# A decoder layer step on one core: gated attention's decays by products from level to level, the decay's input columns loaded once, no arithmetic on GpSimd

## The chip, the cores and the metric

The kernel runs on one core of a Trainium2 chip. The core has TensorE (PE in the profile), VectorE (DVE), ScalarE (ACT), GpSimd (POOL) and SyncE (SP), and 16 DMA engines. Each engine executes its own instructions in order. The metric is the device time of one execution in microseconds; the median of three runs of the kernel before is 2003.5 us (2000.65 to 2004.73).

## The reference, cut to what matters

One layer is computed for 256 prompt tokens and 8 single-token samples, 264 columns in all, with D_MODEL 2048, everything in fp32. The input projection `x @ w_in` gives queries, keys, values, gates and a low-rank (16 columns) input of the decay. The gated attention is the part that the change touches most:

```python
log_a = log_sigmoid(a_lr @ w_gla_a2 + b_gla_a2) / 16.0
...
bc = cumsum(ac, axis=2)                              # log decay, summed over the tokens
decay = exp(where(tri, bc_t - bc_s, -inf))
scores = einsum('bhtk,bhsk,bhtsk->bhts', qc, kc, decay)
o = einsum('bhts,bhsv->bhtv', scores, vc) + einsum('bhtk,bhkv->bhtv', qc * exp(bc), S)
S = exp(b_last) * S + einsum('bhsk,bhsv->bhkv', kc * exp(b_last - bc), vc)
```

The score of tokens t and s is thus the sum over the 256 channels of a head of q_t * k_s * (product of the decays of the tokens after s up to t). There are 4 heads. Beside it run a short gated convolution and a cross-attention into 256 memory tokens; the three are projected, gated and summed, projected by w_o, normed, and followed by a convolutional FFN (D_FF 5504) and a second norm. Each matrix is read once from HBM.

## The kernel before, in words

**Matmuls.** A weight matrix is taken in groups of 512 output columns and granules of two k-tiles (2 x 128 rows, 512 KB). `granule` loads one with a DMA on SP's queue into a staging tile `ws` (4 buffers), casts it on ScalarE into `wh` and takes the remainder on VectorE into `wl` (L277, 3 buffers each). `group` then issues three products for every k-tile and 128 columns, wh·xh, wh·xl and wl·xh (L302 to L304), 264 columns wide and accumulated in PSUM. A granule is 24 such products.

**Order.** After every granule `tick` counts a clock and runs small work that the program has queued: due items of `later(n, f)`, then either a piece of a head's generator (`gens`, a piece ends at a `yield n`, which also says how many ticks the next one waits) or one unit of the queue (`pop`, a unit with loads that were issued two units ahead). Which ticks of a group may do so is one line (L234): with 8 granules those with 5, 4, 2 and 1 granules left, with 4 granules those with 1 and 0 left. All loads of weights and of units go to SP's queue in one order; each waits there for its buffer.

**The places around the change.**
- Memory attention: 16 `key_unit`s multiply a 512 KB piece of the key cache with a row of queries that is read back from DRAM (`dq`, L430) by VectorE (L439); then softmax, `value_unit`s. The prompt's logits (L554), their softmax on VectorE and ScalarE and transposes on TensorE (L568) follow the two memory projections. The projections' results are written to HBM by two DMAs each on GpSimd's queue (L529).
- The decay's input: `group([(win, A0, 32)] * 3, 16, xh, xl, gk=8)` reads the same 32 columns of w_in three times into 96 columns (rows of 128 bytes), in two granules of 8 k-tiles; 48 products.
- `head`: the log decays of a head are summed by a scan (L650); at each of seven lengths l = 1, 2, 4 ... 64 GpSimd subtracts them at the middle of blocks of 2l (L699, L702), ScalarE takes exp (L706), VectorE multiplies with keys and queries (L714, L717), TensorE forms a 128 x 128 product (L679) which VectorE copies where a mask is set (L688). Two more exponents give the decay between the halves and to the end (L736 to L752).
- `sum_rows` (48 calls) transposes 32 x 32 blocks and reduces on VectorE; once in 8 calls `product` sums over four partition groups by four products with shifted identity strips (L473).
- GpSimd also adds `merged` (L1014), the residual (L1087) and a part of the norm's sum (L1135), and its queue loads the FFN's past rows (L1059, two DMAs, rows of 512 bytes).

Of the kernel before, what the change touches and what calls it, by code (L numbers as in the profile page):

```python
# [34 lines left out]
def layer_kernel(ctx, tc, x_prompt, x_sample, mem_prompt, cache_mem_k, cache_mem_v, state_gla, state_conv,  # L35
# [81 lines left out]
    strip = sb.tile([P, 7 * 32], F32, name="strip")  # L117
    vcol = sb.tile([P, NV], F32, name="vcol")
    fcol = sb.tile([P, 172], F32, name="fcol")

    quads = lambda c: strip[:, 96 - 32 * c:224 - 32 * c]

    def constants():
        G.memset(strip, 0.0)
        for a in range(4):
            G.tensor_tensor(strip[:, 96:128], strip[:, 96:128], ident[:, 32 * a:32 * a + 32], ALU.add)
# [102 lines left out]
    def tick(left, n):  # L229

        clock[0] += 1
        with queued_behind():
            due()
            if left in ((1, 0) if n == 4 else (5, 4, 2, 1) if n == 8 and share[2] == 1 else range(2, n)):  # L234
                can = gens and clock[0] >= rest[0]
                if can and (not queue or share[0] < 3):
                    share[0] += 1
                    part()
                elif queue and clock[0] >= share[1]:
                    share[0:2] = [0, clock[0] + share[2]]  # L240
                    pop()
# [217 lines left out]
    def sum_rows(sums, b, z, dst, after=None):  # L459
# [9 lines left out]
        def product():  # L469
            pt = small()  # L470
            o = pt[:, 0:4 * NS].rearrange("p (b j) -> p b j", b=NS)
            for c in range(4):
                T.matmul(o, quads(c), R.rearrange("p b (j c) -> p b j c", c=4)[:, :, :, c], start=(c == 0), stop=(c == 3))  # L473
# [35 lines left out]
    for name, w, dst in (("k", w_mem_k[0], o_mk), ("v", w_mem_v[0], o_mv)):  # L509
# [18 lines left out]
        for m in range(2):  # L528
            G.dma_start(dst[0, 0, m * P:(m + 1) * P].rearrange("m h d -> m (h d)"), mt_[m])  # L529
# [48 lines left out]
    flush()  # L578
# [7 lines left out]
    wr = big(F32, (96, 1024))  # L586
    wa2 = big(F32R, (96, 1024))
    G.memset(wr, 0.0)
    for i in range(3):
        G.dma_start(wr[32 * i:32 * i + 16], w_gla_a2[0])  # L590
    pa, = group([(win, A0, 32)] * 3, 16, xh, xl, gk=8)
    aT = sb.tile([96, NT], F32R, name="aT")
    S.copy(aT, pa[0:96])
# [17 lines left out]
    def head(h, q, k, vf):  # L611
        qk = t2(F32, (P, 2, NP))
        G.tensor_tensor(qk, q[:, :, 0:NP], k[:, :, 0:NP], ALU.mult)
        G.tensor_tensor(qk[:, 0], qk[:, 0], qk[:, 1], ALU.add)
# [13 lines left out]
        def decays_of_samples():  # L628

            S.activation(eas[:, h], la[:, :, NP:NT], AF.Exp, scale=1.0 / 16.0)  # L630
            dot = tiny((P, 2, NS))
            V.tensor_mul(dot, qks[:, 0, h], qks[:, 1, h])
            later(1, lambda: (V.tensor_mul(qas[:, h], qks[:, 0, h], eas[:, h]), own_key(dot)))

        def own_key(dot):
            pz = small()
            for kt in range(2):
                T.matmul(pz[:, 0:NS], onesm, dot[:, kt], start=(kt == 0), stop=(kt == 1))
# [7 lines left out]
        yield 3  # L646

        L = t2(F32, (P, 2, NP))
        for kt in range(2):
            V.tensor_tensor_scan(L[:, kt], smask, la[:, kt, 0:NP], 0.0, ALU.mult, ALU.add)  # L650
        L4 = L.rearrange("p k (c t) -> p (k c) t", t=64)
        Lc = L.rearrange("p k (c t) -> p k c t", t=64)
        D1 = t2(F32, (P, 2, NP))
        D4 = D1.rearrange("p k (c t) -> p (k c) t", t=64)
        Dc = D1.rearrange("p k (c t) -> p k c t", t=64)
        V.tensor_sub(D4, L4[:, :, 63:64].to_broadcast([P, 8, 64]), L4)
        Tc = lambda c: Lc[:, :, c, 63:64]
# [11 lines left out]
        G.memset(sc[:, 3], 0.0)  # L669
# [6 lines left out]
        def gram(E):  # L676
            pg = small()
            for kt in range(2):
                T.matmul(pg[:, 0:P], E[:, kt, 0:P], E[:, kt, P:NP], start=(kt == 0), stop=(kt == 1))  # L679
# [4 lines left out]
        def level():  # L684

            li, E = pending.pop(0)
            pg = gram(E)
            V.copy_predicated(sc[:, 3], masks[:, li], pg[:, 0:P])  # L688

        halves = lambda a: [a[:, :, e * P:(e + 1) * P] for e in range(2)]  # L690

        def exponents(li, l, E):
            blk = lambda a: a.rearrange("p k (b w) -> p k b w", w=2 * l)
            Eh, Lh, qh = ([blk(t) for t in halves(a)] for a in (E, L, q))
            if l < 64:
                Lv = L.rearrange("p k (b w) -> p (k b) w", w=2 * l)
                Ev = E.rearrange("p k (b w) -> p (k b) w", w=2 * l)
                ref = Lv[:, :, l - 1:l].to_broadcast([P, 2 * NP // (2 * l), l])
                G.tensor_tensor(Ev[:, :, 0:l], ref, Lv[:, :, 0:l], ALU.subtract)  # L699
                for e in range(2):  # L700
                    ref = Lh[e][:, :, :, l - 1:l].to_broadcast([P, 2, P // (2 * l), l])
                    G.tensor_tensor(Eh[1 - e][:, :, :, l:2 * l], Lh[e][:, :, :, l:2 * l], ref, ALU.subtract)  # L702

            def decay():
                if l < 64:
                    S.activation(E, E, AF.Exp, scale=1.0 / 16.0)  # L706
                    return
                Ec = E.rearrange("p k (c t) -> p (k c) t", t=64)
                S.activation(Ec[:, 0::2], D4[:, 0::2], AF.Exp, scale=1.0 / 16.0)
                for e in range(2):  # L710
                    S.activation(Eh[1 - e][:, :, 0, l:], Lh[e][:, :, 0, l:], AF.Exp, scale=1.0 / 16.0)

            def products():
                V.tensor_mul(blk(E)[:, :, :, 0:l], blk(E)[:, :, :, 0:l], blk(k[:, :, 0:NP])[:, :, :, 0:l])  # L714
                for e in range(2):
                    u = Eh[1 - e][:, :, :, l:2 * l]
                    V.tensor_mul(u, u, qh[e][:, :, :, l:2 * l])  # L717
                pending.append((li, E))

            later(1, decay)  # L720
            later(2, products)

        for li, l in enumerate(LEVELS):
            yield 1
            exponents(li, l, t2(F32, (P, 2, NP)))
            if len(pending) > 1:
                level()
        yield 2

        E = t2(F32, (P, 2, NP))  # L730
        RD = t2(F32, (P, 2, NP))
        Rc = RD.rearrange("p k (c t) -> p k c t", t=64)
        Ec = E.rearrange("p k (c t) -> p k c t", t=64)
        T23 = tiny((P, 2, 1))
        bc = lambda a: a.to_broadcast([P, 2, 64])
        G.tensor_tensor(T23, Tc(2), Tc(3), ALU.add)  # L736
        G.tensor_tensor(Ec[:, :, 0], Dc[:, :, 0], bc(Tc(1)), ALU.add)
        G.tensor_copy(Ec[:, :, 1], Dc[:, :, 1])
        G.tensor_copy(Ec[:, :, 2], Lc[:, :, 2])
        G.tensor_tensor(Ec[:, :, 3], Lc[:, :, 3], bc(Tc(2)), ALU.add)  # L740
        G.tensor_tensor(RD[:, :, 0:P], E[:, :, 0:P], T23.to_broadcast([P, 2, P]), ALU.add)
        G.tensor_tensor(Rc[:, :, 2], Dc[:, :, 2], bc(Tc(3)), ALU.add)
        G.tensor_copy(Rc[:, :, 3], Dc[:, :, 3])

        def decay_halves():
            S.activation(E, E, AF.Exp, scale=1.0 / 16.0)
            S.activation(RD, RD, AF.Exp, scale=1.0 / 16.0)

# [653 lines left out]
```

## Time and profile before

| what | value |
|---|---|
| runs | 2004.73, 2000.65, 2003.5 us |
| profiled execution, its own time | 2005.06 us |
| its span from first to last instruction | 2003.3 us |
| busy: TensorE, VectorE, ScalarE, GpSimd | 1984.9, 1296.7, 986.3, 164.1 us |
| mean granted TensorE clock | 0.996 |
| VectorE's longest group, the remainders of L277 | 802.6 us in 651 |

A row of the waits reads: engine, tile and line <- what it waited for: us in total, times, the longest. A row of the timeline or of the chain: start in us, duration, engine, line, what. A row of the windows: stretch, its length, then busy us and number of instructions (x) for PE, PEld (weight loads), DVE, ACT and POOL, the granted TensorE clock (1.00 is full), the busy share of the DMA engines, GB/s. In grouped lines "x48 | 5.9, 274" is the count, busy us and mean ns. SPq and POOLq rows are DMA issues; the duration of merged rows ("x2") holds the waits between them.

### The profile page before, as it was taken

What the parts mean: (1) busy time and instruction counts of PE and PEld (TensorE: products, weight loads), DVE (VectorE), ACT (ScalarE), POOL (GpSimd) and SP (SyncE); (2) the same over time, 40 slices, a digit from 0 to 9 for tenths busy, and PEclk for the clock granted to TensorE, in tenths of its full rate; (3) what the DMA queues carried; (4) which work ended last, traced back from release to release, by engine and by line L of the source; (5) the groups of instructions that cost most, each with busy time, mean ns of one, the idle gap of its engine ahead of it and who ended that gap; (6) DMA issues with size and microseconds to landing.
All of it is one profiled execution on the core that took longest, in us unless ns stands there. A gap on an engine that the chain in (4) does not pass through costs nothing.

```text
span 2003.3 us, 38161 instructions
## 1 busy us (share of the span) xinstructions
PE 1984.9 (99%) x15721; PEld 1950.6 (97%) x15721; DVE 1296.7 (65%) x1947; ACT 986.3 (49%) x1348; POOL 164.1 (8%) x240
## 2 busy tenths in 40 slices
PE   9998999999999999999999999999999999999998
PEld 9887999999999999999999998999999999999997
DVE  5675866566676867865444787666665556666655
ACT  4433654454554555554444346555554445555533
POOL 4000030021310211100000201000000000000100
PEclk9999999999999999999999999999999999999999
DMA  8895866566666667866555567877777787777753
GB/s 282 272 316 189 274 201 198 176 211 197 189 190 195 201 190 241 259 173 183 179 179 181 178 213 252 256 236 231 233 246 249 259 254 238 232 233 247 237 177 119
DMA packets 235199, 439.00 MB, mean 219 GB/s; under 512 B 22862, under 2 KB 29571, under 8 KB 234889
## 3 DMA queue, kind: packets, MB, share of 16 engines
q1 hardware_dynamic: 229120, 426.86, 68.9%
q0 software_dynamic: 5040, 8.79, 1.3%
q8 instruction: 123, 2.02, 0.4%
q10 hardware_dynamic: 864, 0.92, 0.1%
q14 instruction: 52, 0.42, 0.1%
HBM read 409.76 MB, written 26.90 MB: 218 GB/s over the span
## 4 chain that ended last, share of the span: by engine, by line
PE 72%; DVE 1%; ACT 0%; issue 0%; DVEq 0%; ACTq 0%
PE mm L303 23%; PE mm L302 23%; PE mm L304 23%; PE sm L803 1%; PE sm L679 0%; PE sm L781 0%; DVE G L935 0%; PE sm L473 0%; PE sm L1276 0%; DVE wl L277 0%; PE sm L849 0%; PE sm L783 0%; PE bank L1331 0%; PE mm L1139 0%; ACT wh L277 0%
## 5 line engine op out<-in xcount | busy, mean ns | idle before, releaser
L277 DVE TENSOR_TENSOR wl<-ws,wh 128x1024 fp32r<-128x1024 f32 (+2 forms) x651 | 802.6, 1234 | 582.0 <-ACT wh L277 580.2
L277 ACT CAST wh<-ws 128x1024 fp32r<-128x1024 f32 (+2 forms) x651 | 676.1, 1039 | 878.0 <-PE mm L303 770.0
L302 PE MATMUL mm<-XH,wh 128*128 128x264 f32 (+1 forms) x2064 | 592.8, 287 | 1.8 <-ACT wh L277 1.0
L303 PE MATMUL mm<-XL,wh 128*128 128x264 f32 (+1 forms) x2064 | 588.8, 286 | 0.0
L304 PE MATMUL mm<-XH,wl 128*128 128x264 f32 (+1 forms) x2064 | 586.2, 285 | 0.7 <-DVE wl L277 0.7
L302 PE MATMUL mm<-T,wh 128*128 128x264 f32 x1456 | 415.1, 285 | 0.0
L303 PE MATMUL mm<-T,wh 128*128 128x264 f32 x1456 | 414.2, 284 | 0.0
L304 PE MATMUL mm<-T,wl 128*128 128x264 f32 x1456 | 413.8, 284 | 0.0
L302 PEld LDWEIGHTS mm<-XH,wh 128*128 128x128 f32 (+1 forms) x2064 | 390.0, 189 | 2.7 <-ACT wh L277 1.2
L302 PE MATMUL mm<-X1H,wh 128*128 128x264 f32 x1376 | 391.5, 284 | 0.0
L303 PE MATMUL mm<-X1L,wh 128*128 128x264 f32 x1376 | 391.1, 284 | 0.0
L304 PE MATMUL mm<-X1H,wl 128*128 128x264 f32 x1376 | 391.0, 284 | 0.0
L303 PEld LDWEIGHTS mm<-XL,wh 128*128 128x128 f32 (+1 forms) x2064 | 389.4, 189 | 0.5 <-DVE XL L317 0.2
L304 PEld LDWEIGHTS mm<-XH,wl 128*128 128x128 f32 (+1 forms) x2064 | 387.8, 188 | 1.2 <-DVE wl L277 1.0
L302 PEld LDWEIGHTS mm<-T,wh 128*128 128x128 f32 x1456 | 274.1, 188 | 0.1
L303 PEld LDWEIGHTS mm<-T,wh 128*128 128x128 f32 x1456 | 274.0, 188 | 0.1
L304 PEld LDWEIGHTS mm<-T,wl 128*128 128x128 f32 x1456 | 273.8, 188 | 0.0
L302 PEld LDWEIGHTS mm<-X1H,wh 128*128 128x128 f32 x1376 | 259.4, 189 | 0.2 <-issue 0.2
L303 PEld LDWEIGHTS mm<-X1L,wh 128*128 128x128 f32 x1376 | 259.0, 188 | 0.2 <-DVE T L1160 0.2
L304 PEld LDWEIGHTS mm<-X1H,wl 128*128 128x128 f32 x1376 | 258.4, 188 | 0.0
L1080 POOL DMA_DIRECT2D out_dram<-S x2 | 1.1, 551 | 637.2 <-DVE S L1077 637.2
L521 PE MATMUL mm<-wl,T 128*128 128x512 f32 x128 | 50.6, 395 | 0.0
(363 smaller groups left out, 1485.7 us busy)
## 6 DMA issues: line engine op xcount, KB each, us to landing
ws<-in_w_in_dram SPq DMA_DIRECT2D x255, 512.0 KB, 4.0
ws<-in_w_ffn_down_dram SPq DMA_DIRECT2D x84, 512.0 KB, 4.8
ws<-in_w_ffn_gate_dram SPq DMA_DIRECT2D x80, 512.0 KB, 4.4
ws<-in_w_ffn_up_dram SPq DMA_DIRECT2D x80, 512.0 KB, 4.7
S<-in_state_gla_dram SPq DMA_DIRECT2D x64, 512.0 KB, 5.3
ws<-in_w_gla_out_dram SPq DMA_DIRECT2D x32, 512.0 KB, 3.7
ws<-in_w_o_dram SPq DMA_DIRECT2D x32, 512.0 KB, 4.2
out_dram<-S SPq DMA_DIRECT2D x32, 512.0 KB, 4.2
```

The costliest lines, as they stand in the source:

```text
L277: split_at[:] = [S.copy(wh, st).ins, V.tensor_sub(wl, st, wh.bitcast(F32)).ins]
L302: T.matmul(p, wh[:, t, cs], xh(kt), start=(kt == 0), stop=False)
L303: T.matmul(p, wh[:, t, cs], xl(kt), start=False, stop=False)
L304: i = T.matmul(p, wl[:, t, cs], xh(kt), start=False, stop=(kt == nk - 1))
L521: T.matmul(pts[m], a, wl[:, t], start=False, stop=False)
L803: T.matmul(pt, kd[:, st, kt * P:(kt + 1) * P], vt[:, st], start=(st == 0), stop=(st == 1))
L1080: G.dma_start(o_pffn[0, 0, u].rearrange("(k f) -> k f", f=P), rows[:, 0])
```

## The change

- **The decay's columns** are loaded once per granule (2 DMAs, not 6). ScalarE spreads the cast to 96 columns, VectorE puts the remainder into columns 96 to 127 of the same tile; the products are one of 128 columns with xh and one of 96 with xl for each k-tile: 32, not 48. The decay's second factor takes 128 rows, so its weights are loaded four times, not three.
- **Decays by products.** The decays themselves are formed by one exp; the scan is gone. Keys and queries carry their decay in place: `lengthen` multiplies, from one level to the next, the keys of the first half of each block and the queries of the second with the decay over the neighbouring half, and keeps the decays of whole blocks in a small table (`wholes`). ScalarE only copies keys and queries side by side for the product of a level.
- **No arithmetic on GpSimd**: merged, residual, the norm's sum, q*k and the zeroing of the scores are on VectorE.
- **sum_rows' product** is one product with an identity summed modulo 32, and the four partition groups are copied out by VectorE and ScalarE in turn. `own_key` adds its two parts on VectorE and needs one product, not two.
- **DMAs**: the memory projections' writes wait 2 and 8 ticks (`later`); the FFN's past rows are loaded by 16 DMAs on SP's queue, two a tick behind a weight load, and their turns come at ticks 14 and 18, not 20 and 24.
- **Ticks**: 6, 4, 2, 1 left with 8 granules, 2 and 1 left with 4; a head's levels are 2 ticks apart, not 1.

```diff
-            if left in ((1, 0) if n == 4 else (5, 4, 2, 1) if n == 8 and share[2] == 1 else range(2, n)):
+            if left in ((2, 1) if n == 4 else (6, 4, 2, 1) if n == 8 and share[2] == 1 else range(2, n)):
...
-            o = pt[:, 0:4 * NS].rearrange("p (b j) -> p b j", b=NS)
+            T.matmul(pt[:, 0:P], modulo.rearrange("p a i -> p (a i)"), R.rearrange("p b c -> p (b c)"),
+                     start=True, stop=True)
+            d = dst() if callable(dst) else dst
             for c in range(4):
-                T.matmul(o, quads(c), R.rearrange("p b (j c) -> p b j c", c=4)[:, :, :, c], start=(c == 0), stop=(c == 3))
-            V.tensor_copy(dst() if callable(dst) else dst, pt[:, 0:4 * NS].rearrange("p (b j) -> p j b", b=NS))
+                own = pt[32 * c:32 * c + 32, 0:P].rearrange("p (b j c) -> p j b c", b=NS, c=4)[:, :, :, c]
+                (S.copy if c % 2 else V.tensor_copy)(d[32 * c:32 * c + 32], own)
...
-            G.dma_start(dst[0, 0, m * P:(m + 1) * P].rearrange("m h d -> m (h d)"), mt_[m])
+            later(2 + 6 * m, lambda dst=dst, mt_=mt_, m=m: G.dma_start(
+                dst[0, 0, m * P:(m + 1) * P].rearrange("m h d -> m (h d)"), mt_[m]))
...
-    pa, = group([(win, A0, 32)] * 3, 16, xh, xl, gk=8)
+    for g in (0, 8):
...
+            staged[:] = [nc.sync.dma_start(
+                st, win[g * P:(g + 8) * P, A0:A0 + 32].rearrange("(k p) c -> p k c", p=P)).ins]
...
+            split_at[:] = [S.copy(wa[:, :, 0:96].rearrange("p k (a c) -> p k a c", a=3),
+                                  st.unsqueeze(2).to_broadcast([P, 8, 3, 32])).ins,
+                           V.tensor_sub(wa[:, :, 96:P], st, wa[:, :, 0:32].bitcast(F32)).ins]
+        for t in range(8):
+            kt = g + t
+            if kt:
+                T.matmul(pa[0:96], wa[:, t, 0:96], xl(kt), start=False, stop=False)
+            i = T.matmul(pa, wa[:, t], xh(kt), start=(kt == 0), stop=(kt == 15))
...
-        for kt in range(2):
-            V.tensor_tensor_scan(L[:, kt], smask, la[:, kt, 0:NP], 0.0, ALU.mult, ALU.add)
...
+        for e in range(2):
+            V.tensor_mul(qx[:, :, (1 - e) * P:(2 - e) * P], q[:, :, e * P:(e + 1) * P], la[:, :, e * P:(e + 1) * P])
...
-                G.tensor_tensor(Ev[:, :, 0:l], ref, Lv[:, :, 0:l], ALU.subtract)
...
+            w = wholes(l)
+            V.tensor_mul(keys[:, :, :, 0:l], keys[:, :, :, 0:l], spread(two(w[:, :, 0:2 * n])[:, :, :, 1], n))
+            V.tensor_mul(queries[:, :, :, l:], queries[:, :, :, l:], spread(two(w[:, :, n:3 * n])[:, :, :, 0], n))
+            V.tensor_mul(wholes(2 * l), two(w)[:, :, :, 0], two(w)[:, :, :, 1])
...
         for li, l in enumerate(LEVELS):
-            yield 1
-            exponents(li, l, t2(F32, (P, 2, NP)))
-            if len(pending) > 1:
+            yield 2
+            E = t2(F32, (P, 2, NP))
+            S.copy(blocks(E, l)[:, :, :, 0:l], blocks(k[:, :, 0:NP], l)[:, :, :, 0:l])
+            S.copy(blocks(E, l)[:, :, :, l:], blocks(qx, l)[:, :, :, l:])
+            later(1, lambda l=l: lengthen(l))
+            if pending:
                 level()
...
-            G.tensor_tensor(merged[c][:, j], merged[c][:, j], sg[:, j], ALU.add)
+            V.tensor_add(merged[c][:, j], merged[c][:, j], sg[:, j])
...
-    for u in range(2):
-        G.dma_start(fr[u * NF:(u + 1) * NF], state_ffn_conv[0, :, u].rearrange("b (k f) -> k b f", f=P))
+    def load_fpast(b):
+        with tc.issue_after(staged[0]):
+            for u in range(2):
+                nc.sync.dma_start(fr[u * NF:(u + 1) * NF, b], state_ffn_conv[0, b, u].rearrange("(k f) -> k f", f=P))
```

What moves, in the engines' own order. SP's queue at the end of the memory projections; `S_...<-in_cache_mem_k` and `T_...<-dq` are a key unit's two loads, `ws<-in_w_in 128x8x32` the decay's columns, `128x2x512` the first query granules. Before:

```order
L428 DMA S_282_1531<-in_cache_mem_k_dram 128x2x512
L270 DMA ws_1818<-in_w_in_dram 128x8x32 x3
L270 DMA ws_1866<-in_w_in_dram 128x2x512
L430 DMA T_283_1533<-dq 128x512
L270 DMA ws_1896<-in_w_in_dram 128x2x512
L428 DMA S_291_1561<-in_cache_mem_k_dram 128x2x512
L270 DMA ws_1926<-in_w_in_dram 128x2x512
L270 DMA ws_1974<-in_w_in_dram 128x2x512
L430 DMA T_292_1563<-dq 128x512
```

The same place on SP's queue with the change:

```order
L427 DMA S_279_1511<-in_cache_mem_k_dram 128x2x512
L429 DMA T_280_1513<-dq 128x512
L601 DMA ws_1804<-in_w_in_dram 128x8x32
L427 DMA S_291_1559<-in_cache_mem_k_dram 128x2x512
L269 DMA ws_1842<-in_w_in_dram 128x2x512
L429 DMA T_292_1561<-dq 128x512
L269 DMA ws_1872<-in_w_in_dram 128x2x512
```

The last row of queries stands behind one query granule, where it stood behind four. TensorE's order after the decay's products, before (`L568` are the transposes of the prompt's first softmax):

```order
L304 MATMUL mm_1785<-XH,wl_1823 96x264
L302 MATMUL mm_1862<-XH,wh_1868 128x264
L568 MATMUL sm_1675<-ident,T_320_1670 128x128 x4
L554 MATMUL sm_1681<-T_209_1243,T_46_428 128x256 x4
L303 MATMUL mm_1862<-XL,wh_1868 128x264
```

With the change, the last nine of 13 such products of the queries, and what stands behind them:

```order
L302 MATMUL mm_1838<-XL,wh_1844 128x264
L303 MATMUL mm_1838<-XH,wl_1845 128x264
L301 MATMUL mm_1839<-XH,wh_1844 128x264
L302 MATMUL mm_1839<-XL,wh_1844 128x264
L303 MATMUL mm_1839<-XH,wl_1845 128x264
L301 MATMUL mm_1839<-XH,wh_1844 128x264
L302 MATMUL mm_1839<-XL,wh_1844 128x264
L303 MATMUL mm_1839<-XH,wl_1845 128x264
L301 MATMUL mm_1840<-XH,wh_1844 128x264
L571 MATMUL sm_1671<-ident,T_320_1666 128x128 x4
L557 MATMUL sm_1677<-T_209_1239,T_46_428 128x256 x4
```

The transposes (now L571) stand behind 13 products of the queries, where they stood behind one. The FFN's past rows on SP's queue, where before only weight loads stood:

```order
L269 DMA ws_12715<-in_w_o_dram 128x2x512
L1056 DMA S_1805_12706<-in_state_ffn_conv_dram 43x128 x2
L269 DMA ws_12747<-in_w_o_dram 128x2x512
L1056 DMA S_1805_12706<-in_state_ffn_conv_dram 43x128 x2
L269 DMA ws_12779<-in_w_o_dram 128x2x512
```

There are eight such pairs, in the first of w_o's four groups.

More of the change, by code (lines that the diff above doesn't have):

```diff
@@ L577, in layer_kernel @@
                 split(omh[c][:, 2 * hh + d, 0:NP], oml[c][:, 2 * hh + d, 0:NP], pt[:, 0:NP])
-    flush()
+    while queue:
+        pop()
     put(None, softmax_unit)
@@ L686, in level @@
             li, E = pending.pop(0)
-            pg = gram(E)
+            pg = gram(E, E, P)
             V.copy_predicated(sc[:, 3], masks[:, li], pg[:, 0:P])
[L690 to L698, printed above, removed]
-                G.tensor_tensor(Ev[:, :, 0:l], ref, Lv[:, :, 0:l], ALU.subtract)
-                for e in range(2):
[L701 to L721, printed above, removed]
@@ L733, in head @@
[L733 to L741, printed above, removed]
@@ L1057, in layer_kernel @@
     fr = s4((2 * NF, NS, P))
[L1058 to L1059 removed]
+    def load_fpast(b):
+        with tc.issue_after(staged[0]):
+            for u in range(2):
+                nc.sync.dma_start(fr[u * NF:(u + 1) * NF, b], state_ffn_conv[0, b, u].rearrange("(k f) -> k f", f=P))
+    for b in range(NS):
+        later(1 + b, lambda b=b: load_fpast(b))
     def turn_fpast(b0):
```

114 lines of the change are left out of this document (61 added, 53 removed).

## The prediction

> **What bounds the kernel now.** I read the page's busy times first, then TensorE's waits, then its clock by stretches.
>
> ```profile
> PE 1984.9 (99%) x15721; PEld 1950.6 (97%) x15721; DVE 1296.7 (65%) x1947; ACT 986.3 (49%) x1348; POOL 164.1 (8%) x240
> ...
> PE sm L568 <- ACT wh L277: 6.3, 1, 6.3
> PE mm L302 <- ACT wh L277: 1.0, 1, 1.0
> PE mm L304 <- DVE wl L277: 0.7, 1, 0.7
> PE mm L302 <- DVE G L985: 0.7, 1, 0.7
> PE sm L568 <- DVE T L564: 0.4, 2, 0.2
> ...
> 160.00:164.00 4.00, 0.97 (x9) 0.76 (x7) 0.43 (x3) 0.00 (x0) 0.00 (x0) 1.00 1.05 303
> 168.00:173.00 5.00, 5.00 (x17) 4.28 (x16) 2.98 (x5) 0.00 (x0) 0.00 (x0) 0.51 0.69 211
> 835.00:845.00 10.00, 10.00 (x83) 9.93 (x82) 9.12 (x13) 6.53 (x8) 3.55 (x4) 1.00 0.73 215
> 870.00:880.00 10.00, 8.27 (x54) 7.85 (x53) 4.52 (x5) 3.14 (x3) 0.00 (x0) 0.83 0.58 168
> ```
>
> TensorE is busy for 99% of the span: whatever shortens its work shortens the kernel, and work on other engines counts only where TensorE waits for it. In the middle of the program it waits at three places, for 6.3, 1.0 + 0.7 and 0.7 us. After the first two the granted clock is half: 0.51 over 168 to 173, and 0.83 over 870 to 880, where 10 us undisturbed hold 83 instructions and this stretch 54. A wait thus costs more than its length. So I count products taken away, then ask of each wait whether the change removes its cause.
>
> **The change part by part.** *Products.* The pitch of the decay's products comes from the second and the last of the 48:
>
> ```profile
> 154.96 0.28 PE L303 MATMUL mm<-XL,wh 128*96 128x264 f32 x1
> ...
> 160.57 0.28 PE L304 MATMUL mm<-XH,wl 128*96 128x264 f32 x1
> ...
> 567.12 0.44 PE sm L679 x4
> 579.70 0.82 PE sm L473 x8
> 657.21 0.34 PE sm L638 x4
> ```
>
> 46 steps in 5.61 us are 0.122 us each (the 0.28 overlap); 16 fewer save 16 x 0.122 = 1.95 us. The chain shows that an fp32 product is two pieces: two of 128 x 128 take 0.44 us, so one takes 0.22; the four with the strips take 0.82. `sum_rows` closes six times: 6 x (0.82 - 0.22) = 3.6 us. `own_key` halves 0.34 us, four times: 0.7 us. Together **6.2 us**, certain to within 0.5. A head still forms seven levels, the product between halves and its transposes, so nothing else on TensorE changes in number.
>
> *The wait at L568.* It is a late transfer. SP, VectorE and TensorE around it:
>
> ```profile
> 148.36 0.47 SPq L430 DMA_DIRECT2D T<-dq  x1
> ...
> 151.40 0.96 DVE L277 TENSOR_TENSOR wl<-ws,wh 128x768 fp32r<-128x768 f32 x1 [1.80 <-ACT wh L277]
> ...
> 149.91 2.85 SPq L270 DMA_DIRECT2D ws<-in_w_in_dram  x2
> ...
> 152.81 0.46 SPq L430 DMA_DIRECT2D T<-dq  x1
> ...
> 163.57 0.42 DVE L439 SCALAR_TENSOR_TENSOR T<-S,T 128x256 f32<-128x256 f32 x1 [6.18 <-DMA T<-dq]
> ...
> 167.25 1.09 PE L568 MATMUL sm<-ident,T 128*128 128x128 f32 x4 [6.28 <-ACT wh L277]
> ...
> ws<-in_w_in_dram SPq DMA_DIRECT2D x6, 128.0 KB, 5.9
> ...
> out_dram<-T POOLq DMA_DIRECT2D x2, 512.0 KB, 7.7
> ```
>
> The last row of queries is issued at 152.81, because the weight load ahead of it waits for its buffer until the split begun at 151.40 is done, and lands at 163.5 in a DMA that is full (share 1.05). VectorE sits 6.18 us on it, with the softmax queued behind; 3.7 us later (163.57 to 167.25) the transposes start. The change takes away four of the six loads in rows of 128 bytes, lets the two 512 KB writes wait, and moves the row of queries ahead of three weight loads. Its place is then the one that stood before 148.36 in the old queue, at least 4.5 us earlier. Ahead of it stand a key piece, a weight granule and itself, 512 + 512 + 256 KB; at the 303 GB/s of the row at 160 that takes 4.3 us: landed near 153. The bounds are 4 us in an empty queue and the 10.7 us seen, 152.4 to 159.1. TensorE comes to the transposes about where it did: 16 products fewer, 12 more queries' products ahead, -4 x 0.122 = -0.5 us, at 160.3. With 3.7 us behind the landing the transposes are ready between 156 and 162.8; I take the near end, since the traffic that filled the DMA is what goes. The softmax itself then stands next; its two short waits (0.4 us in all) show how close it runs, so I leave 0.5 us there. What goes is 6.3 us and the half clock behind it, 5.0 x 0.49 + 0.75 x 0.5 = 2.8 us: **9.1 us**, less 0.5.
>
> *The wait at 873.* GpSimd's loads of the FFN's past rows come just before:
>
> ```profile
> 849.67 5.29 POOL L1059 DMA_DIRECT2D S<-in_state_ffn_conv_dram  x2 [11.12 <-DVE T L817]
> ...
> ws<-in_w_in_dram SPq DMA_DIRECT2D x11, 512.0 KB, 8.2
> S<-in_state_ffn_conv_dram POOLq DMA_DIRECT2D x2, 172.0 KB, 19.5
> ...
> ws<-in_w_in_dram SPq DMA_DIRECT2D x255, 512.0 KB, 4.0
> ...
> 874.75 0.39 PE L302 MATMUL mm<-XH,wh 128*128 128x264 f32 x1 [0.98 <-ACT wh L277]
> ...
> 876.01 0.59 PE L304 MATMUL mm<-XH,wl 128*128 128x264 f32 x1 [0.75 <-DVE wl L277]
> ```
>
> While 344 KB in rows of 512 bytes take 19.5 us to land, a weight granule takes 8.2 us where 4.0 is usual, and casts come late. The change sends these rows in 16 pieces of 22 KB through SP, later, in w_o's first group, two behind a weight load. SP pays 2 x 0.47 us (the row at 148.36) in each 2.9 us granule beside one weight issue of that size, and weights are four buffers ahead: nothing. What goes is 0.98 + 0.75 us of waiting and, by the clock of 0.83, 10 x 0.17 = 1.7 us: **3.4 us**. If the pieces disturb the weights as the old loads did, nothing is won here. [...]
>
> *GpSimd's arithmetic.* One VectorE instruction is stretched sevenfold while GpSimd works, and TensorE's third wait follows it:
>
> ```profile
> 660.84 3.52 DVE L935 SCALAR_TENSOR_TENSOR G<-G,vcol,G 128x255 f32<-128x255 f32 x1
> ...
> 665.49 0.47 DVE L935 SCALAR_TENSOR_TENSOR G<-G,vcol,G 128x255 f32<-128x255 f32 x1
> ...
> L1012 DVE TENSOR_TENSOR G<-G,mm 128x264 f32<-128x264 f32 x16 | 6.1, 419 | 0.1
> ...
> L1095 DVE SCALAR_TENSOR_TENSOR T<-T,T 128x1056 f32<-128x1056 f32 x3 | 3.7, 1257 | 0.0
> ...
> L714 DVE TENSOR_TENSOR T<-T,T 128x256 f32<-128x256 f32 x28 | 13.9, 498 | 0.0
> ```
>
> Without arithmetic there, **0.7 us** of waiting goes. VectorE takes over 16 x 0.419 (merged), 4 x 1.257 (residual), 3 x 0.419 (norm), and 4 x about 1.2 for q*k: 18 us, against the scan and subtractions it loses; a level stays at two products of 256 elements plus a small one for the table, 1.0 to 1.3 us. With 700 us idle on VectorE that is hidden while `wl` is ready in its three buffers. The norm's sum is on the path to the FFN: three adds on VectorE delay its own next add by up to 1.2 us, against GpSimd's stretched ones; between 0.5 lost and 0.5 won, I take nothing. ScalarE swaps exps for copies of the same length. The ticks only move small work: nothing.
>
> **The sum.** 6.2 + 9.1 - 0.5 + 3.4 + 0.7 = 18.9 us. The profiled span of 2003.3 becomes 1984.4; that execution's own time is 2005.06, but the median of the runs shown, 2003.5, lies 0.2 above the span. Forecast: **1984.6 us**.
>
> **The rivals.** A measurement of this kernel tells 0.2%, 4 us, from no change.
> - *The transposes still wait* (chance 0.14). For it: VectorE's own queue there is full of splits, and a landing at 159.1 is allowed above. Against: 6.18 us of VectorE's idling name the transfer. At worst all 9 us stay: 1993.7.
> - *Another wait takes the place of the one at 873* (0.10): the 16 pieces, or a unit at a new tick. [...] One such wait with its half clock is 3.4 us: 1988.
> - *VectorE becomes the bound of the heads* (slower, 0.05). In a group of four granules VectorE has 11.6 us.
>
> ```profile
> L277 DVE TENSOR_TENSOR wl<-ws,wh 128x1024 fp32r<-128x1024 f32 x627 | 781.4, 1247 | 566.8 <-ACT wh L277 565.2
> ...
> L465 DVE STREAM_TRANSPOSE T<-T 128x512 f32<-128x512 f32 x48 | 34.0, 708 | 0.9
> L467 DVE TENSOR_REDUCE T<-T 128x16 f32<-128x512 f32 x48 | 32.7, 680 | 0.9
> L817 DVE SCALAR_TENSOR_TENSOR T<-S,qas,T 128x512 f32<-128x512 f32 x32 | 25.9, 811 | 1.5 <-ACT T L816 1.3
> ```
>
> Splits 4 x 1.25, a sum unit of 0.81 + 0.71 + 0.68, a level (1.3, and 0.3 for its masked copy as an estimate from the smallest of these) and evictions of 4 x 0.42 are 10.5. If the strided products ran at three times the row of L714, 2.0 more, it would be 12.5, over 11.6, and each of 28 levels could bring a late split. At 3.4 us each, six cost 20.4 and the gain is gone; from seven on, 2008, the kernel is slower, and ten give 2019. Against: VectorE's 65%.
> - *Small waits eat the gain* (0.04), in the same way but five of them: 1984.6 + 17 = 2002, no change that can be told.
>
> The forecast has 0.67. Faster 0.91 (0.67 + 0.14 + 0.10), the same 0.04, slower 0.05. The range reaches from 1980 (the spread of the runs, 2 to 3 us, the 0.5 not needed, two more stretched splits gone) to 1994, where the transposes wait in full; what is left out is the last two rivals and a few hundredths at the edges.
>
> **What would show it.** In the changed kernel's profile: L473's successor at 0.22 us and 32 products for the decay; no idle before L571 over 1 us and a clock of 1.00 from 150 to 180; the last `dq` landed before 157; no wait and clock 1.00 around 870; VectorE's L935 group at 0.48 us throughout. The forecast is wrong if a half-clock stretch remains between the start and the last 20 us, or if TensorE waits for `wl` in the heads.

## The result, and the profile after

The changed kernel takes 1988.1 us (median of 5 runs, 1987.73 to 1988.67); the kernel before, beside it on the same chip, 2001.75 us (5 runs, 2000.65 to 2004.73). The ratio is 0.9928, 95% interval [0.9914, 0.9941]: 13.7 us faster, where 18.9 were forecast. The profiled execution took 1987.76 us with a span of 1985.7, so the two profiled spans differ by 17.6 us.

The page's busy row of the changed kernel, then TensorE's waits, then stretches of the span (columns: length; busy time and count of PE, PEld, DVE, ACT, POOL; granted clock; DMA share; GB/s):

```profile
PE 1973.7 (99%) x15661; PEld 1939.0 (98%) x15661; DVE 1282.4 (65%) x1995; ACT 976.2 (49%) x1365; POOL 44.3 (2%) x95
```

```profile
PE warm L108 <- DVE ones L97: 1.1, 1, 1.1
...
PE sm L901 <- DVE ty L659: 0.7, 1, 0.7
PE mm L301 <- ACT T L886: 0.7, 1, 0.7
PE sm L571 <- DVE T L567: 0.5, 2, 0.3
...
PE sm L571 <- ACT wh L276: 0.4, 2, 0.2
```

```profile
160.00:164.00 4.00, 3.72 (x25) 3.46 (x25) 3.24 (x6) 0.25 (x1) 0.00 (x0) 1.00 1.06 346
168.00:173.00 5.00, 5.00 (x28) 4.53 (x28) 3.10 (x5) 1.48 (x4) 0.00 (x0) 1.00 0.68 199
835.00:845.00 10.00, 10.00 (x85) 10.00 (x84) 4.84 (x4) 4.44 (x5) 0.00 (x0) 1.00 0.65 200
870.00:880.00 10.00, 10.00 (x84) 10.00 (x83) 6.26 (x8) 4.39 (x8) 0.00 (x0) 1.00 0.67 196
```

All three waits of the old list are gone (the transposes of the softmax, L568 before, are L571 now), and the granted clock is 1.00 where it was 0.51 and 0.83. What the transposes still wait is 0.5 + 0.4 us in four pieces, none over 0.3. TensorE is busy 11 us less, in 60 instructions fewer. There are two waits in the middle of the program that the old list did not have, 0.7 us each: one for the values' copies (L886), and one of the transposes of the samples' values (L901), which the list puts down to a small tile of `own_key` (L659). Both lie at 372 to 376 us.

The row of queries and VectorE's first instruction on it, which the argument on L568 was about:

```profile
144.84 0.47 SPq L429 DMA_DIRECT2D T<-dq  x1
...
149.65 0.42 DVE L438 SCALAR_TENSOR_TENSOR T<-S,T 128x256 f32<-128x256 f32 x1 [1.02 <-DMA T<-dq]
```

It is issued 8 us earlier than before and is used at 149.65, 4.8 us after its issue where it took 10.8 before; VectorE waits 1.02 us for it in place of 6.18.

The new waits, in ScalarE's order of time, and TensorE's instruction behind them:

```profile
366.62 0.65 ACT L650 ACTIVATE T<-T 128x528 f32<-128x528 f32 x1
...
367.90 1.28 ACT L651 ACT_TABLE_LOAD   x1
369.19 0.65 ACT L651 ACTIVATE T<-T 128x528 f32<-128x528 f32 x1
369.74 1.04 ACT L276 CAST wh<-ws 128x1024 fp32r<-128x1024 f32 x1
370.80 1.28 ACT L655 ACT_TABLE_LOAD   x1
372.09 0.64 ACT L655 ACTIVATE T<-T 128x528 f32<-128x528 f32 x1
372.64 0.36 ACT L886 COPY T<-mm 128x264 f32<-128x264 f32 x1
...
373.06 0.39 PE L301 MATMUL mm<-XH,wh 128*128 128x264 f32 x1 [0.66 <-ACT T L886]
```

The second head's decays (exp L650, log L651, exp L655, with two loads of ScalarE's function table of 1.28 us among them) run just when ScalarE should empty the PSUM tiles of a group of values. ScalarE's first copy comes at 372.64, and TensorE, which needs the tile for its next group, waits for it. The second new wait, with VectorE's order ahead of it:

```profile
373.98 1.23 DVE L276 TENSOR_TENSOR wl<-ws,wh 128x1024 fp32r<-128x1024 f32 x1 [0.24 <-ACT wh L276]
375.12 0.17 DVE L887 COPY vs<-T 128x32 f32<-128x32 f32 x1
...
375.45 0.60 PE L901 MATMUL sm<-ident,vs 128*32 128x128 f32 x4 [0.67 <-DVE ty L659]
```

The tile that L901 reads is `vs`, which the copy L887 fills; the copy stands behind a split of 1.23 us, and L659 runs right after it. The product of `own_key` itself comes only at 378.80 and waits for nothing.

### The profile page after: what moved, and what is told of

It reads as the page before. It is cut to its first block, busy times and chain, and to the rows that moved or that the text cites. A ratio compares the mean times of both kernels' runs of the same rounds, so it can differ in the third digit from the quotient of the medians.

```text
span 1985.7 us, 37900 instructions
## 1 busy us (share of the span) xinstructions
PE 1973.7 (99%) x15661; PEld 1939.0 (98%) x15661; DVE 1282.4 (65%) x1995; ACT 976.2 (49%) x1365; POOL 44.3 (2%) x95
## 4 chain that ended last, share of the span: by engine, by line
PE 97%; DVE 1%; ACT 1%; DMA 0%; issue 0%; ACTq 0%; DVEq 0%
PE mm L302 30%; PE mm L301 30%; PE mm L303 29%; PE mm L523 1%; PE mm L524 1%; PE mm L522 1%; PE sm L712 1%; ACT wh L276 0%; DVE wl L276 0%; PE sm L578 0%; PE sm L775 0%; PE sm L557 0%; DMA T<-in_x_prompt_dram 0%; PE sm L777 0%; PE sm L697 0%; PE sm L386 0%
## 5 line engine op out<-in xcount | busy, mean ns | idle before, releaser
L276 DVE TENSOR_TENSOR wl<-ws,wh 128x1024 fp32r<-128x1024 f32 (+2 forms) x649 | 785.4, 1211 | 565.4 <-ACT wh L276 563.7
L301 PE MATMUL mm<-XH,wh 128*128 128x264 f32 x2048 | 587.1, 287 | 0.7 <-ACT T L886 0.7
L302 PE MATMUL mm<-XL,wh 128*128 128x264 f32 x2048 | 582.6, 285 | 0.0
L303 PE MATMUL mm<-XH,wl 128*128 128x264 f32 x2048 | 580.4, 284 | 0.0
L301 PEld LDWEIGHTS mm<-XH,wh 128*128 128x128 f32 x2048 | 386.4, 189 | 1.1 <-ACT T L886 0.9
L302 PEld LDWEIGHTS mm<-XL,wh 128*128 128x128 f32 x2048 | 385.7, 188 | 0.5 <-DVE XL L316 0.2
L303 PEld LDWEIGHTS mm<-XH,wl 128*128 128x128 f32 x2048 | 384.0, 188 | 0.3 <-DVE wl L276 0.2
L524 PE MATMUL mm<-wh,T 128*128 128x512 f32 x128 | 50.5, 394 | 0.0
```

The source lines that it names most:

```text
L276: split_at[:] = [S.copy(wh, st).ins, V.tensor_sub(wl, st, wh.bitcast(F32)).ins]
L301: T.matmul(p, wh[:, t, cs], xh(kt), start=(kt == 0), stop=False)
L302: T.matmul(p, wh[:, t, cs], xl(kt), start=False, stop=False)
L303: i = T.matmul(p, wl[:, t, cs], xh(kt), start=False, stop=(kt == nk - 1))
L524: i = T.matmul(pts[m], b, wh[:, t], start=False, stop=(kt == 15))
```

## The experiments

None of the kernels below leaves anything of the computation out. `before` stands for the kernel before, run beside each; its medians in the three comparisons were 2002.24 (21 runs), 2003.18 (9) and 2001.62 (23).

| run | what it is | median us (range) | ratio to before, 95% interval |
|---|---|---|---|
| b_cols | before + columns loaded once | 1992.46 (1992.32 to 1994.75) | 0.9951 [0.9937, 0.9965] |
| b_fpast | before + FFN's past rows through SP | 2000.33 (1997.05 to 2003.33) | 0.9988 [0.9980, 0.9997] |
| b_prod | before + fewer small products | 1996.44 (1992.57 to 1997.66) | 0.9962 [0.9949, 0.9976] |
| b_nopool | before + decays by levels, no GpSimd arithmetic | 2000.52 (1998.54 to 2002.99) | 0.9991 [0.9982, 1.0000] |
| a_cols3 | after, columns loaded three times | 1995.86 (1994.28 to 1998.42) | 0.9966 [0.9953, 0.9978] |
| a_writes | after, writes at once | 1988.08 (1987.50 to 1989.19) | 0.9925 [0.9912, 0.9939] |
| a_ticks | after, old ticks | 1984.51 (1984.38 to 1984.78) | 0.9907 [0.9894, 0.9921] |
| a_best | after, values' copies on VectorE | 1987.48 (1987.00 to 1988.20) | 0.9922 [0.9910, 0.9935] |
| a_t8 | after, old ticks in groups of 8 alone | 1985.15 (1984.57 to 1986.01) | 0.9917 [0.9904, 0.9930] |
| b_ticks | before + new ticks | 2002.34 (1999.53 to 2006.43) | 1.0005 [0.9997, 1.0014] |
| b_again | before, a second profile | 2001.69 (1998.50 to 2002.83) | 0.9996 [0.9988, 1.0005] |
| t_pool | a_ticks with some adds on GpSimd | 1984.97 (1984.15 to 1986.04) | 0.9916 [0.9903, 0.9929] |

The first four each do one part of the change alone; then parts are undone in the changed kernel, to find what removed the wait at L568 and what the new wait costs.

### b_cols: the columns' loads alone

```diff
-    pa, = group([(win, A0, 32)] * 3, 16, xh, xl, gk=8)
+    # one load of 32 columns per 8 k-tiles, copied three times on ScalarE; 32 products
```

> The kernel before with one part of the change: the decay's columns loaded once (32 products instead of 48). The prediction's theory: the late row of queries comes from the loads in rows of 128 bytes and from what they push behind them on SP, so the wait of 6.3 us at the softmax's transposes goes with its half clock: 2.0 us of products and 5 to 9 us of waiting, 7 to 11 us faster. Rival (the writes of the memory projections, or the ticks, make the row late): the wait stays at 4 us or more and only the products go, 2 to 3 us faster.

9.8 us faster than before. The row of queries and the waits in it:

```profile
145.66 0.47 SPq L430 DMA_DIRECT2D T<-dq  x1
```

```profile
PE mm L304 <- DVE wl L277: 0.7, 1, 0.7
PE mm L302 <- DVE G L1005: 0.7, 1, 0.7
PE sm L568 <- DVE T L564: 0.5, 2, 0.3
```

The row is issued at 145.66, without any change in the ticks or in the writes, and the wait of 6.3 us is gone. This part alone removes it.

### a_cols3: the reverse

```diff
-    # one load of 32 columns per 8 k-tiles
+    pa, = group([(win, A0, 32)] * 3, 16, xh, xl, gk=8)
```

> The changed kernel, but with the decay's columns loaded three times and split into wh and wl as before (48 products at the decay instead of 32). Theory (the three-fold loads of 128-byte rows by themselves make the last row of dq late): the wait at L571 comes back with 3 to 7 us, with half clock behind it or without, and the 16 products come back with 2.0 us, so 6 to 10 us above the changed kernel: 1994 to 1998. Rival (the deferred 512 KB writes and the earlier loads of weights, which this kernel keeps, are what lets dq land in time): no wait at L571, only the 2 us of products: 1990.

7.8 us above a_writes, which ran beside it and equals the changed kernel (1995.86 against 1988.08). SP's queue, VectorE behind it, and TensorE's wait:

```profile
142.60 5.86 SPq L269 DMA_DIRECT2D ws<-in_w_in_dram  x4
148.51 0.47 SPq L429 DMA_DIRECT2D T<-dq  x1
...
153.06 0.46 SPq L429 DMA_DIRECT2D T<-dq  x1
...
164.26 0.43 DVE L438 SCALAR_TENSOR_TENSOR T<-S,T 128x256 f32<-128x256 f32 x1 [7.25 <-DMA T<-dq]
```

```profile
PE sm L571 <- ACT wh L276: 7.4, 1, 7.4
```

With new ticks and deferred writes, but the old loads, the last row goes out at 153.06, as before, and lands as late. The rival, that ticks and writes let it land in time, falls. Ahead of the row at 148.51 four loads, three of them the columns', hold SP's queue for 5.86 us, the waits between them included. The last row is used 14.6 us later than in the changed kernel: 8.2 of these are its later issue, and 6.4 a slower transfer (11.2 us after the issue, not 4.8). What slows the transfer was not separated. This profile is of the longest of the five executions, 1998.42 us, so its wait of 7.4 us is not that of the median.

### a_writes: the projections' writes at once

```diff
-            later(2 + 6 * m, lambda ...: G.dma_start(dst[...], mt_[m]))
+            G.dma_start(dst[...], mt_[m])
```

> The changed kernel with the projections' two 512 KB writes issued at once again, in place of 2 and 8 ticks later. Theory (the columns' loads alone were the cause): dq still lands ahead of its transposes, no wait over 0.5 us at L571, the time unchanged within 1 us: 1987.5 to 1989. Rival (the writes fill the DMA engines when dq comes): a wait of 2 to 6 us at L571, 1990 to 1996.

1988.08 against 1988.1 us, and the transposes wait 0.6 + 0.4 us in four pieces, none over 0.3. Deferring the writes does nothing that can be measured.

### b_fpast: the FFN's past rows through SP

```diff
-        G.dma_start(fr[...], ...)            # two, 172 KB each, early
+        nc.sync.dma_start(fr[...], ...)      # sixteen of 22 KB, behind weight loads
```

> The kernel before with one part of the change: the FFN's past rows loaded by 16 DMAs on SP's queue instead of two on GpSimd's, with their turns at ticks 14 and 18. The prediction's theory: the waits near 873 of 1.73 us and the half clock behind them go, nothing comes in their place: 3.4 us faster in the profile, 1.5 to 3.5 in the median of the runs if not every run of the kernel before falls into half clock there. Rival (the small pieces disturb the weights as the two large loads did): no change, and a wait appears in w_o's first group.

1.9 us faster. Two waits and the stretch at 870:

```profile
PE sm L568 <- ACT wh L277: 6.7, 1, 6.7
```

```profile
870.00:880.00 10.00, 10.00 (x85) 10.00 (x84) 5.40 (x8) 4.52 (x5) 0.00 (x0) 1.00 0.65 191
```

The wait at 873 is gone and TensorE waits nowhere between 845 and 1200, so the sixteen small pieces harm nothing. They are worth less in the median than the 3.4 us of the profile: see b_again.

### b_prod: the small products

```diff
-            for c in range(4): T.matmul(o, quads(c), R[...c], ...)
+            T.matmul(pt[:, 0:P], modulo, R, start=True, stop=True)
```

(and the same for `own_key`, whose two products become one.)

> The kernel before with one part of the change: the product that ends sum_rows is one of 128 x 128 instead of four of 32 columns, copied out in four parts, and own_key takes one product instead of two. The prediction's theory: 3.6 + 0.7 = 4.3 us faster, by TensorE's time alone. Rival (these small products lie in gaps where TensorE waits anyway, or the four copies are waited for): under 1.5 us.

5.8 us faster, 1.5 more than expected. What one product costs now shows in the changed kernel's TensorE:

```profile
765.19 0.39 PE L471 MATMUL sm<-T,modulo 128*128 128x128 f32 x2
765.33 0.37 PE L301 MATMUL mm<-XH,wh 128*128 128x264 f32 x1
```

The next product starts 0.14 us later; six such places measure 0.14 four times and 0.22 twice, against 0.81 before. (After the 0.14, as after the 0.81, the product that follows starts another 0.09 late, so the difference stands.) `own_key` went from 0.36 to 0.14, four times. Together 3.9 + 0.9 = 4.8 us. The profile of this kernel also has a shorter wait:

```profile
PE sm L571 <- ACT wh L277: 3.3, 1, 3.3
```

```profile
165.00:168.00 3.00, 3.00 (x19) 2.79 (x20) 2.36 (x3) 0.11 (x1) 0.00 (x0) 1.00 1.06 411
168.00:173.00 5.00, 4.69 (x40) 4.51 (x39) 3.33 (x7) 2.07 (x5) 0.00 (x0) 1.00 0.51 156
```

3.3 us where the profile of before has 6.3, and no half clock behind it. But the profiled execution is the fastest of five, 1992.57 us; a second took 1992.85, the other three 1996.44 to 1997.66. So the profile shows why that execution is short; where the 1.0 us of the median beyond the 4.8 comes from is not shown.

### b_nopool: the heads by levels, GpSimd idle

```diff
-        G.tensor_tensor(qk, q, k, ALU.mult)      # and the subtractions on GpSimd, the scan on VectorE
+        V.tensor_mul(qk, q, k)                   # and products of two halves, level by level
```

> The kernel before with one part of the change: the heads with decays by products, and merged, residual and the norm's sum added on VectorE, no arithmetic on GpSimd in the stages. The prediction's theory: 0.7 us of waiting goes, and a wait of about 1.3 us that the changed kernel shows near 373 (copies of the values behind exps with table loads on ScalarE) comes: between 1 us faster and 2 us slower. Rival A (VectorE's stretched instructions cost TensorE more than the one wait shows): 2 to 5 us faster. Rival B (VectorE bounds the heads): over 4 us slower.

1.7 us faster, with an interval that ends at 1.0000: more than the theory's 1 us and less than the 2 of rival A, and the interval allows both. TensorE's waits:

```profile
PE sm L568 <- ACT wh L277: 4.4, 1, 4.4
PE mm L302 <- DVE G L981: 1.4, 1, 1.4
PE mm L521 <- DVE wl L277: 1.3, 1, 1.3
```

L521 is at 120.9 us, in the memory projections. L981, at 795.6, falls into the time of the last head, but VectorE isn't full there: ScalarE idles 3.63 us for a late weight load at 789.50, and VectorE 1.33 us before the split at 793.93 that stands ahead of L981. So VectorE carries the extra work of the heads without loss. The old wait of 0.7 us for L985 is gone, and the wait expected near 373 did not come. The wait at 873 is absent here too. GpSimd's two loads of the past rows are still made, but 76 us earlier, at 773 and 776 us: before, the last adds of `merged` stood ahead of them in GpSimd's queue until 838.6. They land at 792 and 797 us, where the wait of 1.4 us now stands. That they cause it was not tested by itself; the profiles below speak for it.

### b_again: the kernel before once more

> The kernel before, unchanged, for a second profile of it. Theory (the size of the waits at 160 and at 873 us, and whether half clock follows, differ between executions): the wait at L568 is between 3 and 7.5 us, and the waits at 873 us differ from 1.0 + 0.7 us by more than 0.3 us; the times scatter over 4 us or more. Rival (the waits belong to the program and come out alike): 6.3 and 1.7 us again, within 0.3, and the scatter lies elsewhere.

2001.69 us, 1998.50 to 2002.83. Its waits and two stretches:

```profile
PE sm L568 <- ACT wh L277: 5.6, 1, 5.6
...
PE mm L304 <- DVE wl L277: 0.7, 1, 0.7
```

```profile
165.00:168.00 3.00, 2.11 (x7) 1.92 (x8) 1.70 (x4) 1.02 (x2) 0.00 (x0) 0.50 0.91 290
...
870.00:880.00 10.00, 9.26 (x75) 8.83 (x74) 6.43 (x9) 5.71 (x6) 0.00 (x0) 1.00 0.74 225
```

The same program waits 5.6 us here in place of 6.3, and at 873 only 0.7 us without half clock, where the first profile had 1.7 us of waiting and 3.4 us of half clock. The first profile is of an execution of 2005.06 us, this one of 2000.33. The size of both waits, and the clock behind them, differs between executions of one program; the changed kernel has neither wait, and its five runs lie within 1 us. The second wait follows the loads of the past rows: it ends at 874.8 us with the loads issued at 849.7 (before), at 872.9 with 847.2 (here), at 867.8 with 844.4 (b_ticks), at 864.6 with 839.2 (b_cols) and at 795.6 with 773.2 (b_nopool), 22 to 26 us behind each time. Only b_prod, with the loads at 841.4, has no wait there; so the loads bring it in most executions, not in all.

### a_best: the values' copies on VectorE

```diff
-                    (S.copy if j % 2 else V.tensor_copy)(vf[:, j], pv[j])
+                    V.tensor_copy(vf[:, j], pv[j])
...
-            later(1, lambda: (..., own_key(dot)))
+            later(2, lambda: (..., own_key(dot)))
```

> The changed kernel with the four copies of the values (L886) all on VectorE in place of two on ScalarE, and own_key one tick later. Theory (the new wait at 372 us is the value copies queued on ScalarE behind two loads of its function table, 1.28 us each, and the key's product queued behind VectorE's split): the wait of 1.84 us goes or falls under 0.5, the time 1.3 to 1.8 us lower than the changed kernel's: 1986.3 to 1986.8. Rival (VectorE is itself late there, since its split of 1.22 us stands between the copies): the wait stays, with VectorE as its releaser, 1988.

1987.48 us: 0.6 lower, where 1.3 to 1.8 were expected, and the two kernels' runs overlap. The wait on the copies is gone, the other one is longer:

```profile
PE sm L901 <- DVE vs L887: 1.0, 1, 1.0
```

It was in VectorE's queue already; the samples' values (L887) now stand behind a split of 1.23 us and a reduction of 0.68. The theory took this wait for that of the key's product, which waits for nothing. Giving the copies to the other engine removes one wait and lengthens the other.

### a_ticks and a_t8: the ticks

```diff
-            if left in ((2, 1) if n == 4 else (6, 4, 2, 1) if ...
+            if left in ((1, 0) if n == 4 else (5, 4, 2, 1) if ...       # a_ticks
+            if left in ((2, 1) if n == 4 else (5, 4, 2, 1) if ...       # a_t8
```

> The changed kernel with the old ticks, (1, 0) in groups of 4 and (5, 4, 2, 1) in the groups of 8, in place of (2, 1) and (6, 4, 2, 1). Theory (the ticks only shift when the side work is issued, and VectorE and ScalarE have room): within 1 us of the changed kernel, 1987 to 1989. Rival (the later tick is what brought the new wait of 1.8 us at 372 us): that wait goes, 1986 to 1986.5. Second rival (the ticks are what keeps the splits ahead of their matmuls): several waits of L304 on wl of 0.5 to 1.5 us, 1990 to 1993.

> The changed kernel with (5, 4, 2, 1) in place of (6, 4, 2, 1) in the groups of 8 alone; the groups of 4 keep (2, 1). Theory (the first tick of the groups of 8 sets where the second head's decays fall: at 366.6 us, on the value copies of 370 to 374 us, with 6; at 405.8 us, far from them, with 5): the decays go back to about 406 us, no wait at 372 us, 1984.2 to 1985. Rival (the groups of 4 sum up to that shift, so that the heads start a group later): the decays stay near 366 us with the wait of 1.8 us, 1987.5 to 1988.5.

a_ticks takes 1984.51 us, 3.6 below a_writes beside it, and their runs don't overlap: the fastest version here, 0.9907 [0.9894, 0.9921] of before. That is further than any theory put it. Its waits, and ScalarE's order:

```profile
PE warm L108 <- DVE ones L97: 1.1, 1, 1.1
...
PE sm L571 <- DVE T L567: 0.6, 2, 0.3
```

```profile
364.76 0.38 ACT L886 COPY T<-mm 128x264 f32<-128x264 f32 x1 [0.53 <-PE mm L303]
...
405.84 0.65 ACT L650 ACTIVATE T<-T 128x528 f32<-128x528 f32 x1
...
412.25 0.65 ACT L655 ACTIVATE T<-T 128x528 f32<-128x528 f32 x1
```

The decays of the second head run at 405.84 in place of 366.62, and the values' copies at 361 to 367 meet nothing. Between the memory attention and the norm before the FFN no wait is listed any more. a_t8 reverts only the groups of 8: its decays run at 403, the wait at 372 is gone, and it takes 1985.15 us; its runs overlap with those of a_ticks. So the first tick of the groups of 8 (6 in place of 5) is what brought the wait. Of the 3.6 us, the traces place 2.0 between 200 and 850 us, where the two waits of 0.7 at 372 lie; 0.5 stands before 20 us, where the input is loaded, and 0.9 is spread over 950 to 1220 us in steps too small to name. Another 0.3 lies outside the span (an execution takes 2.1 us more than its span in the changed kernel, 1.7 here). What makes up the 2.2 us beside the two waits stays open.

### b_ticks: the ticks in the kernel before

```diff
-            if left in ((1, 0) if n == 4 else (5, 4, 2, 1) if ...
+            if left in ((2, 1) if n == 4 else (6, 4, 2, 1) if ...
```

> The kernel before with the ticks (2, 1) and (6, 4, 2, 1) alone. Theory (a tick costs only through what the moved work meets; the order of before has no decays on the value copies at 380 to 384 us, but may get them there): if the second head's decays move onto the copies, a wait of 1 to 2 us comes and the time rises by 1 to 4 us, 2003 to 2007; if they don't, within 1.5 us of before. Rival (the ticks help the row of dq to land earlier): the wait at L568 falls from 6 us to under 3 and the time by 3 us or more, 2000 or less.

No change that can be told, 1.0005 [0.9997, 1.0014]; the second head's decays stay behind the values' copies (387 us against 376 to 380), and there is no wait there. The new ticks cost nothing by themselves, only with the new lengths of the heads' pieces. The wait at L568 is 4.4 us in this profile, and 3.3 to 6.7 us over the kernels that keep the old loads; that the ticks shorten it is not shown, and the time does not fall.

### t_pool: some adds back on GpSimd

```diff
-            V.tensor_add(merged[c][:, j], merged[c][:, j], sg[:, j])
+            G.tensor_tensor(merged[c][:, j], merged[c][:, j], sg[:, j], ALU.add)
```

(and the adds of the residual and of the norm; with the old ticks.)

> The changed kernel with the old ticks (which took 1984.5 us) and, besides, the adds of merged, of the residual and of the norm back on GpSimd. Theory (those adds are few and TensorE waits for none of them): within 0.7 us of it, 1984 to 1985.2. Rival (VectorE's instructions are stretched while GpSimd works, and a late split follows): one or more waits of L304 or L302 for DVE of 0.5 us or more, 1985.5 to 1988.

1984.97 against 1984.51 us, no change. Two splits of VectorE beside GpSimd's adds:

```profile
1093.03 6.42 DVE L276 TENSOR_TENSOR wl<-ws,wh 128x1024 fp32r<-128x1024 f32 x2 [0.39 <-ACT wh L276]
```

The two take 6.42 us where 1.2 each is usual, and TensorE waits for nothing between 1080 and 1110 us: the three buffers of `wl` cover it.

## Why the prediction was right, and where it was off

The forecast was 1984.6 us within 1980 to 1994; the result, 1988.1, is 3.5 us above it. The span came out 1985.7 for 1984.4, which is 1.3 of it. The other 2.2 lie in the last line of the sum, where the median of the runs "lies 0.2 above the span": the changed kernel's median lies 2.4 above its span. An execution's own time is 1.8 us above its span before and 2.1 after; the 0.2 came from setting the span of one of the longest executions (2005.06) against the median of the others. Its gain, with longer waits to lose, was larger than that of a median execution for the same reason. That the kernel without the new ticks takes 1984.51 us, just the forecast, is luck: its span is 1982.7, so the terms together were 1.7 us too small, and the step from span to median hides it. Of these 1.7, 0.5 are the small products; the rest was not traced.

- **Products**, 6.2 forecast. 4.8 measured for the small ones (4.3 forecast), since the successor comes 0.14 to 0.22 us later. The decay's sixteen are not isolated in any run; in the changed kernel's trace thirty of the products start 3.64 us apart (154.59 to 158.23), 0.121 each, which gives 1.94 for sixteen.
- **The wait at L568**, 9.1 less 0.5. Right in cause and, for that execution, in size: b_cols removes it by the loads alone (9.8 us, 7.9 without the products' 1.95), a_cols3 brings back a wait of 7.4 us. The prediction named three causes side by side and did not weigh them. That the change "lets the two 512 KB writes wait" did not matter, as a_writes shows; that it "moves the row of queries ahead of three weight loads" is not a cause of its own, since in a_cols3 and b_cols the row's place in SP's queue follows the loads of the columns, not the ticks. The landing was put near 153 within 152.4 to 159.1; the row is used at 149.65, below both bounds, as it was issued at 144.84 and not just before 148.36. This error did no harm, since TensorE reached the transposes at 160.1, as forecast (160.3). The residual, 0.5 forecast, is 0.5 + 0.4, against 0.4 before: right.
- **The wait at 873**, 3.4. It is gone. b_fpast removes it by the past rows alone, and the wait follows their loads from profile to profile; b_prod, which keeps the old loads, has none either, so one profile without it would not be proof. The size holds for the profiled execution; the second profile of before waits 0.7 us there at full clock, and b_fpast gains 1.9 us in the median.
- **GpSimd's arithmetic**, 0.7. The third wait is gone, in b_nopool too. That VectorE's other work hides is confirmed by b_nopool. The group that had the stretched instruction is even in the changed kernel, 479 ns on average for 853 before:

```profile
L929 DVE SCALAR_TENSOR_TENSOR G<-G,vcol,G 128x255 f32<-128x255 f32 x8 | 3.8, 479 | 0.0
```
- **The ticks**, "only move small work: nothing". This is the step that failed. They brought the waits of 0.7 + 0.7 us at 372, and a_ticks is 3.6 us faster without them. The rival "another wait takes the place of the one at 873" had named "a unit at a new tick" and priced it to 1988; it gave the time, though neither the place (372 us, not 873) nor the price (no half clock there) as it was put, so that the time agrees is luck.

That the four parts alone sum to 9.8 + 1.9 + 5.8 + 1.7 = 19.2 us, and the whole is worth 13.7, is for the most part the ticks: without them the change is worth 2003.18 - 1984.51 = 18.7, the same within the parts' intervals. VectorE as the bound of the heads did not come; no list of TensorE's waits after the change has `wl` in the heads.

## What to carry to other kernels

A wait's length in one profile belongs to that execution (the same program waited 6.3 us at L568 in one and 5.6 in another, and 1.7 and 0.7 at 873): before it goes into a sum against a median, set the profiled execution's own time against the runs, and take a second profile if they differ. An edit of the order that moves "only small work" is to be followed to the engine's queue that it lands in: here two loads of ScalarE's function table of 1.28 us each, two exps and a log of 0.65 fell in front of the copies that free TensorE's PSUM tiles. And where a transfer is late, look for what occupies its queue ahead of it as well as for the traffic beside it: here the issue made 8.2 of 14.6 us.

## What had not been expected of the hardware

In these runs the half clock does not follow the length of the wait. Behind 3.3 us of waiting there was none (b_prod), while in the profile of before 1.7 us at 873 were followed by 3.4. And two kernels that both waited 4.4 us at L568 differ in it; b_nopool, then b_ticks:

```profile
165.00:168.00 3.00, 1.85 (x7) 1.71 (x8) 1.70 (x5) 1.28 (x3) 0.00 (x0) 0.50 1.05 387
168.00:173.00 5.00, 5.00 (x27) 4.46 (x26) 2.38 (x4) 0.87 (x4) 0.00 (x0) 0.71 0.77 247
```

```profile
165.00:168.00 3.00, 3.00 (x10) 2.35 (x8) 1.82 (x2) 0.00 (x0) 0.00 (x0) 0.51 1.03 378
168.00:173.00 5.00, 4.70 (x39) 4.49 (x38) 3.06 (x6) 2.07 (x5) 0.00 (x0) 1.00 0.42 111
```

In the first the clock is half until 170.9 us (0.71 over 168 to 173 is 2.9 us of it), in the second until 167.9; in both it is still 1.00 over 160 to 164.

In the profile of before the granted clock is 1.00 up to 166.07 us, 0.50 to 172.90, 1.00 to 876.05, 0.50 to 879.46, 1.00 to 1995.62 and 0.50 from there to the end of the span. The four stretches between these changes are 6.83, 703.15, 3.41 and 1116.16 us long, that is 2, 206, 1 and 327 times 3.413 us. In three other runs the granted clock of stretches around 165 us gives half stretches of about 6.8 us (b_again, b_fpast) and 10.2 (a_cols3), close to two and three times that length. Five steps of 3.41 us in the profile of before:

| step of before, us | idle share of TensorE | clock of the next step |
|---|---|---|
| 159.25 to 162.66 | 0.50 | full |
| 162.66 to 166.07 | 1.00 | half |
| 872.63 to 876.05 | 0.51 | half |
| 1988.79 to 1992.21 | 0.19 | full |
| 1992.21 to 1995.62 | 0.16 | half |

A step idle for half its length was followed by full clock once and by half once, and near the end half clock came after 0.16, where 0.19 had been followed by full; the changed kernel's clock is 1.00 up to 1977.32 and half from there, after 3.41 us that were idle for 0.26. So in these profiles neither the length of a wait nor the idle share of one step tells whether half clock follows. What decides it was not shown.
